# Hyena filter spectra: the even/odd sums on TensorE, one store per side, and the second layer's modulations emitted between the gate blocks

## The chip, the cores and the metric

One core of a Trainium2 chip. The metric is the device time of one execution in microseconds; before, the median of three runs is 1911.43 us (1908.09 to 1912.96). Beside it stands one profiled execution, whose trace all rows below come from.

## The reference

A two-layer diffusion trunk over 1024 latent tokens and 256 context tokens of width 1024. Layer 0 mixes neighbourhood attention and a bidirectional gated DeltaNet behind one input projection. Layer 1 is an order-2 Hyena layer: two long convolutions whose filters come from a small network. Only a part of it is touched here:

```python
def hyena_filters(length, w1, b1, f1, w2, b2, f2, w3):
    ...
    hid = jnp.sin(f2 * (hid @ w2 + b2))
    h = (hid @ w3).astype(jnp.float32).reshape(length, HY_ORDER, HY_DIRS, HY_W)
    ...
    h = h * jnp.exp(-t * decay)[:, None, None, :]
    return h * lax.rsqrt(jnp.sum(h * h, axis=0, keepdims=True) + EPS)

def long_conv(u, h_fwd, h_bwd, skip):
    ...
    hf = jnp.fft.rfft(h_fwd, n=n, axis=0)
    hb = jnp.fft.rfft(h_bwd, n=n, axis=0)
```

Each layer also has a modulation, `m = silu(cvec) @ mod_w + mod_b`, split into shift, scale and gate, and layer 0 a gate path, `silu(px[..., OFF_Z:])`.

## The kernel before, in words

The program is recorded through a scheduling layer that orders each engine's instructions itself, by priority and by its own estimate of when operands are ready; every engine then executes its row in that order. The work of the change lies in `start` (from L317), the first fifth of the program.

**Filter blocks.** For each of 8 channel blocks cb and 2 orders o, so 16 blocks, `filter_pair` (L1259) makes the filters `fh` from the hidden layer by TensorE, multiplies them by the decay on VectorE and normalises them. `filter_block` (L1299) forms the sum and the difference of the forward and the backward filter, folds them into even and odd parts with VectorE and GpSimd, and transposes them with TensorE into `fx` (`xT` in the code). `filter_spectrum` (L1323) is a discrete Fourier transform by matrix products, for a cosine side (0) and a sine side (1). Per side a product `e[:, 0]` of the even samples and a product `e[:, 1]` of the odd ones go into one PSUM bank, and four smaller products into a second bank `r`. ScalarE copies `e[:, 0]` to SBUF (L1340), VectorE makes its sum and its difference with `e[:, 1]` (L1341, L1342), then adds and subtracts the first two parts of `r` (L1343, L1344); ScalarE copies the rest (L1345, L1349). Both sides of a block lie in one SBUF tile `G`, of which there is one; two stores (L1350, L1351) take it to `g_d`, where the second layer reads it much later. The spectra's banks come from pool psf, of three.

**Fill.** With the lowest priority, so that it fills gaps, `start` also records the last four blocks of layer 0's modulation (em), eight gate blocks z0 to z7 (`zblock`, L475) and the twelve blocks of layer 1's modulation, om0 to om11 (`mod_block`, L200). A z block loads 512 KB of weights, ScalarE makes a high part and a negated copy of them, a DMA of GpSimd's queue adds the weights onto the negated copy to give the low part (`load_split` with add, L145), 24 products follow, and ScalarE (L486) and VectorE (L487) empty the bank. A modulation block loads two tiles of 512 KB, makes 8 narrow products, has ScalarE copy the result (L213), and then either transposes it (om0 to om7) or makes one more product (om_g, L224), to which VectorE adds a bias row that SP has just loaded (L226, L227) before a store (L228). All fill shares one PSUM bank (pool psz) and the weight places wraw, whi and wlo, two of each.

**What follows.** `layer0_in` for the second half of the tokens (transposes `xtp1`, VectorE's `xmod`), then `project` (L408): `gates` (L564) makes products `ab` with the small weights `wab`, which are loaded through the same places, and `dn_front` makes the DeltaNet projections `dn` (weights `wdn`).

Of the kernel before, what the change touches and what calls it, by code (L numbers as in the profile page):

```python
# [10 lines left out]
F32 = mybir.dt.float32  # L11
# [3 lines left out]
AF = mybir.ActivationFunctionType  # L15
ALU = mybir.AluOpType
# [4 lines left out]
P = 128  # L21
# [26 lines left out]
Z_EARLY = range(8)  # L48
# [13 lines left out]
class Kernel:  # L62
# [44 lines left out]
    def mm3(self, ps, ws, xs, start, stop):  # L107
        nc = self.nc
        (wh, wl), (xh, xl) = ws, xs
        nc.tensor.matmul(ps, wh, xh, start=start, stop=False)  # L110
        nc.tensor.matmul(ps, wh, xl, start=False, stop=False)  # L111
        nc.tensor.matmul(ps, wl, xh, start=False, stop=stop)  # L112
# [204 lines left out]
    def start(self, st, sh, h):  # L317

        nc, ap = self.nc, self.ap
        psp = self.pool(st, "fpsg", bufs=2, space=bass.MemoryType.PSUM)  # L320
        pst = self.pool(st, "fpst", bufs=2, space=bass.MemoryType.PSUM)
        psf = self.pool(st, "fpsf", bufs=3, space=bass.MemoryType.PSUM)
        self.psg = self.pool(st, "psz", bufs=1, space=bass.MemoryType.PSUM)
        mp = self.pool(st, "mp")
        fc = self.pool(st, "fc")
        self.mod_setup(mp)
        fw = self.pool(st, "fw", bufs=2)
        self.wraw = self.pool(sh, "wraw", bufs=2, side="right")
        self.wsp = self.pool(sh, "wsp", bufs=2, side="right")
        self.ev = self.pool(sh, "ev", bufs=3, side="right")  # L330
        self.hpool(sh, h, 0, 512)
        self.hpool(sh, h, 2, LC)
        self.pending = [None, None]
        with ExitStack() as s1:
            fa = self.fa = self.pool(s1, "fa", side="right")
            hid = [fa.tile([P, L], F32R, name="fhh"), fa.tile([FFN, L], F32R, name="fhl")]
            self.ffn(mp, fw, psp, *hid)
            for j in range(8):
                if j == CONST_AT:
                    w3 = [self.load_w3(0)]  # L340
                    fil = hid, *self.filter_setup(fc)
                self.mod_block(mp, "em", j, self.cols0, None, pst)
            xs = self.load_x(0)
            for cb in range(KT):
                if cb == X_AT:
                    self.layer0_in(xs, psf, h[0], 0, "f")
                    with self.tc.high_priority(offset=-LOW):
                        for j in range(8, 12):
                            self.mod_block(mp, "em", j, None, self.gate_d[0:1, :])
                        for zb in Z_EARLY:  # L350
                            self.zblock(h, zb, (0,), add=True)
                        for j in range(12):
                            self.mod_block(mp, "om", j, self.cols1, self.gate_d[1:2, :])
                if cb == X2_AT:
                    self.layer0_in(self.load_x(2), psf, h[2], 2, "f")
                if cb == X1_AT:
                    xs = self.load_x(1)
                self.filter_pair(cb, w3.pop(0), fil, pst, psp, psf, fw)
                if cb + 1 < KT:
                    w3.append(self.load_w3(cb + 1))  # L360
            self.flush(0)
        self.hpool(sh, h, 1, 512)
        self.layer0_in(xs, pst, h[1], 1)
        self.flush(1)
# [877 lines left out]
    def filter_setup(self, fc):  # L1242

        nc, ap = self.nc, self.ap
        trow = self.fa.tile([P, L], F32, name="trow")
        nc.sync.dma_start(trow, ap["trow"])
        ndel = fc.tile([P, KT], F32, name="ndel")
        nc.sync.dma_start(ndel, ap["ndelta"])
        skip = fc.tile([P, 2, KT], F32, name="skip")
        nc.sync.dma_start(skip, ap["skip"])  # L1250
        mats = self.load_dft(fc, ("a0", "a1", "b0", "b1", "co", "so", "cc", "ss0", "ccn"))
        return trow, ndel, skip, mats

    def load_w3(self, cb):
# [68 lines left out]
    def filter_spectrum(self, cb, o, xTs, mats, psf, fw):  # L1323
        nc = self.nc
        nm = f"{cb}_{o}"
        G = fw.tile([P, 2, 10, P], F32, name="G" + nm, tag="G", bufs=1)
        v = nc.vector
        for side in (1, 0):
            xT = xTs[side]
            e = psf.tile([P, 2, 2, P], F32, name=f"fb0{nm}_{side}", tag="f")  # L1330
            r = psf.tile([P, 4, P], F32, name=f"fb1{nm}_{side}", tag="f")
            m0, m1, mo, mc = ("a0", "a1", "co", "cc") if side == 0 else ("b0", "b1", "so", "ss0")
            self.dft([e[:, 0]], mats[m0], [xT[:, 0:2, :]])
            self.dft([e[:, 1]], mats[m1], [xT[:, 2:4, :]])
# [7 lines left out]
            v.tensor_tensor(Gs[:, 5::4, :], t, e[:, 1], ALU.subtract)  # L1342
            v.tensor_tensor(Gs[:, 0:2, :], Gs[:, 8:10, :], r[:, 0:2], ALU.add)  # L1343
            v.tensor_tensor(Gs[:, 2:4, :], Gs[:, 8:10, :], r[:, 0:2], ALU.subtract)  # L1344
            nc.scalar.copy(Gs[:, 6:8, :], r[:, 2:4])  # L1345
            if side == 0:
                b2 = psf.tile([P, P], F32, name=f"fb2{nm}", tag="f")
                self.dft([b2], mats["ccn"], [xT[:, 6, :], xT[:, 8, :]])
                nc.scalar.copy(G[:, 0, 8, :], b2)  # L1349
        nc.sync.dma_start(self.g_d[o, cb][:, 0:16, :].rearrange("p (a b) c -> p a b c", a=2), G[:, :, 0:8, :])  # L1350
# [312 lines left out]
class Conv:  # L1663
# [284 lines left out]
```

## Time and profile before

| | us |
|---|---|
| median of the timed runs | 1911.43 |
| the profiled execution | 1918.28 |
| span of its trace, first to last instruction | 1916.5 |
| mean granted TensorE clock | 0.955 of full |
| first and last instruction on a spectrum's bank | 85.0 and 383.9 |
| z products, first z block to last modulation product | 111.4 to 349.1 |
| first product with wab, first DeltaNet product | 384.0, 394.9 |

PE is TensorE's products, PEld its weight loads, DVE VectorE, ACT ScalarE, POOL GpSimd, SP the engine whose queue issues most DMAs. Busy time of PE includes products that ran at a lower granted clock and so took longer. A product of fp32 operands is two instructions in the trace. In a row of waits, the left side waited for the right; in a row of the timeline the square brackets say how long the engine had been idle and what ended it. A helper records many operations at one line (L116 for products, L105 and L102 for splits), so groups are told apart by their tiles.

### The profile page before, as it was taken

The page shows a single profiled execution, that of the slowest core. Times are in us where ns is not written, and L with a number is a line of the kernel's source. Part 1 is how long each engine was busy: PE and PEld are TensorE (multiplying, and loading weights), DVE is VectorE, ACT ScalarE, POOL GpSimd, SP SyncE. Part 2 cuts the span into 40 slices and gives each one's busy share as a digit, 9 for nine tenths or more (in the row PEclk, how much of TensorE's full clock was granted, in tenths as well). Part 3 has the DMA queues.
Part 4 walks back from the last instruction along what each step waited for, and adds up shares of the span by engine and source line. Part 5 has one row for each costly group of instructions (what it writes and reads, how often), then busy time and mean ns, then how long its engine had stood idle before and what let it go on. Part 6 is the DMA issues. An engine that isn't in the chain of part 4 may idle for free.

```text
span 1916.5 us, 30316 instructions
## 1 busy us (share of the span) xinstructions
PE 1744.8 (91%) x11124; PEld 1417.4 (74%) x11124; DVE 1405.9 (73%) x2818; ACT 836.7 (44%) x1817; POOL 627.8 (33%) x878
## 2 busy tenths in 40 slices
PE   6798988799989897999987999989999999999898
PEld 2466755678877686888876787778888778888686
DVE  5899988746658554655565765659899989999876
ACT  4557574445535342333344544544334434434321
POOL 0665445422295768721035400330000000000410
PEclk9889988999999998999998999999999999999999
DMA  8535545213424366434489872643343442443343
GB/s 288 173 110 152 158 162 177 98 62 102 158 73 138 122 209 229 150 122 160 150 228 207 228 204 85 185 116 90 105 111 85 106 111 68 111 128 110 106 132 136
DMA packets 131934, 270.50 MB, mean 141 GB/s; under 512 B 43929, under 2 KB 65961, under 8 KB 129738
## 3 DMA queue, kind: packets, MB, share of 16 engines
q1 hardware_dynamic: 122330, 233.45, 37.6%
q0 software_dynamic: 9456, 35.13, 9.6%
q8 instruction: 87, 1.43, 0.3%
q14 instruction: 61, 0.50, 0.1%
HBM read 192.50 MB, written 76.03 MB: 140 GB/s over the span
## 4 chain that ended last, share of the span: by engine, by line
PE 58%; DVE 21%; DMA 8%; POOL 4%; ACT 3%; issue 3%; SPq 1%; DVEq 0%; ACTq 0%; POOLq 0%
PE hx L116 6%; PE fo L116 4%; PE hg L116 3%; PE pa L116 3%; PE hu L116 3%; PE nv L116 2%; DVE ff L1160 2%; PE nq L116 2%; PE z L116 2%; PE pv L116 2%; PE pq L116 2%; PE nk L116 2%; PE do L116 2%; POOL sub L755 2%; POOL Xb L757 2%
## 5 line engine op out<-in xcount | busy, mean ns | idle before, releaser
L112 PE MATMUL dn<-hh,wdn_lo 128*128 128x512 f32 (+1 forms) x256 | 96.0, 376 | 5.9 <-POOL wdn_lo L105 5.9
L652 DVE SCALAR_TENSOR_TENSOR dacc<-dpad,convw,dacc 128x1024 f32<-128x1024 f32 (+1 forms) x80 | 83.7, 1078 | 23.8 <-ACT dacc L650 19.0
L116 PE MATMUL hx<-h1l,w1x_hi 128*128 128x512 f32 x256 | 101.1, 395 | 0.0
L116 PE MATMUL hx<-h1h,w1x_hi 128*128 128x512 f32 x256 | 101.0, 395 | 0.0
L116 PE MATMUL hx<-h1h,w1x_lo 128*128 128x512 f32 x256 | 100.9, 394 | 0.0
L111 PE MATMUL dn<-hl,wdn_hi 128*128 128x512 f32 (+1 forms) x256 | 95.7, 374 | 0.0
L110 PE MATMUL dn<-hh,wdn_hi 128*128 128x512 f32 (+1 forms) x256 | 95.6, 374 | 0.0
L755 POOL TENSOR_TENSOR sub<-Lb,Xb 80x31 f32<-80x31 f32 (+15 forms) x124 | 80.2, 647 | 34.9 <-DMA Lb<-lsc_d 21.2
L757 POOL TENSOR_TENSOR Xb<-Xb,sub 80x31 f32<-80x31 f32 (+15 forms) x124 | 82.3, 664 | 8.4
L1051 ACT ACTIVATE pr<-pr,st 128x640 f32<-128x640 f32 (+1 forms) x64 | 51.4, 803 | 64.9 <-DVE st L1050 64.3
L112 PEld LDWEIGHTS dn<-hh,wdn_lo 128*128 128x128 f32 x256 | 49.4, 193 | 14.9 <-POOL wdn_lo L105 6.1
L1171 ACT COPY fx<-fx_ps 128x512 f32<-128x512 f32 (+1 forms) x96 | 43.5, 483 | 30.9 <-PE fx_ps L121 27.6
L121 PE MATMUL fx_ps<-ident,ff 128*128 128x128 f32 x288 | 51.2, 305 | 5.8 <-ACT fx L1171 3.6
L1280 PE MATMUL fh<-fhh,w3s 128*128 128x512 f32 x64 | 38.9, 611 | 18.4 <-DVE fh L1282 18.4
L110 PEld LDWEIGHTS dn<-hh,wdn_hi 128*128 128x128 f32 x256 | 49.5, 193 | 7.9
L111 PEld LDWEIGHTS dn<-hl,wdn_hi 128*128 128x128 f32 x256 | 49.3, 193 | 8.1 <-issue 0.5
L116 PEld LDWEIGHTS hx<-h1h,w1x_hi 128*128 128x128 f32 x256 | 48.1, 188 | 9.0
L116 PEld LDWEIGHTS hx<-h1l,w1x_hi 128*128 128x128 f32 x256 | 48.1, 188 | 8.9
L116 PEld LDWEIGHTS hx<-h1h,w1x_lo 128*128 128x128 f32 x256 | 48.2, 188 | 8.9
L1304 POOL TENSOR_TENSOR fp<-fh,fh 128x1024 f32<-128x1024 f32 x16 | 39.4, 2461 | 41.6 <-ACT fh L1290 25.2
L121 PEld LDWEIGHTS fx_ps<-ident,ff 128*128 128x128 f32 x288 | 37.5, 155 | 19.9 <-ACT fx L1171 6.6
L116 PE MATMUL hu<-h1h,w1u_hi 128*128 128x512 f32 x128 | 51.3, 401 | 0.8 <-ACT hpu L1631 0.8
(570 smaller groups left out, 5952.2 us busy)
## 6 DMA issues: line engine op xcount, KB each, us to landing
hG<-g_d SPq DMA_DIRECT2D x16, 1088.0 KB
g_d<-G SPq DMA_DIRECT2D x16, 1024.0 KB
em_w<-in_em_w SPq DMA_DIRECT2D x24, 512.0 KB
om_w<-in_om_w SPq DMA_DIRECT2D x24, 512.0 KB
wz_raw<-in_w0z SPq DMA_DIRECT2D x16, 512.0 KB
w1x_raw<-in_w SPq DMA_DIRECT2D x16, 512.0 KB
w1x_lo<-in_w POOLq DMA_DIRECT2D x16, 512.0 KB, 7.7
wdn_raw<-in_w0dn SPq DMA_DIRECT2D x12, 512.0 KB
```

Source lines behind the costliest of these rows:

```text
L110: nc.tensor.matmul(ps, wh, xh, start=start, stop=False)
L111: nc.tensor.matmul(ps, wh, xl, start=False, stop=False)
L112: nc.tensor.matmul(ps, wl, xh, start=False, stop=stop)
L116: ins = self.nc.tensor.matmul(*args, **kw)
L121: ins = self.nc.tensor.transpose(out, x, self.ident)
L652: nc.vector.scalar_tensor_tensor(acc[:, t0:t0 + n], pad[:, o + j:o + j + n], cw[:, blk, j:j + 1], acc[:, t0:t0 + n], ALU.mult, ALU.add)
L755: nc.gpsimd.tensor_tensor(tv, Lb[:, j + 1:, j:j + 1].broadcast_to([80, m, c]), Xb[:, j:j + 1, 0:c].broadcast_to([80, m, c]), ALU.mult)
L757: nc.gpsimd.tensor_tensor(Xb[:, j + 1:, 0:c], Xb[:, j + 1:, 0:c], tv, ALU.subtract)
L1051: nc.scalar.activation(pr[:, :n], pr[:, :n], AF.Exp, bias=st[:, 0:1], scale=-1.0, accum_out=st[:, 1:2])
L1171: nc.scalar.copy(out[:, j0:j0 + m, :].rearrange("p a b -> p (a b)"), ps[:, :m * P])
L1280: nc.tensor.matmul(ps, ws[:, od, :], hh[:, sl], start=True, stop=False)
L1304: nc.gpsimd.tensor_tensor(pp[:, :L], hf[:, :L], hb[:, :L], ALU.add)
```

## The change

Three edits. In `filter_spectrum` the sum and the difference of the even and the odd product are formed in PSUM: `e[:, i]` accumulates the even product and then the odd one with the matrix `a1` (or `b1`) for i = 0, and with its negative for i = 1. Two negated matrices are made once. ScalarE copies one part of both results straight to G and the other to `t`, and VectorE keeps the two operations with `r`. G is a tile per side, each stored on its own. In `start`, two modulation blocks of layer 1 are recorded ahead of each of the first six gate blocks, not all twelve behind the eighth.

```diff
-                        for zb in Z_EARLY:
+                        for i, zb in enumerate(Z_EARLY):
+                            for j in range(2 * i, min(2 * i + 2, 12)):
+                                self.mod_block(mp, "om", j, self.cols1, self.gate_d[1:2, :])
                             self.zblock(h, zb, (0,), add=True)
-                        for j in range(12):
-                            self.mod_block(mp, "om", j, self.cols1, self.gate_d[1:2, :])
...
+        for name in ("a1", "b1"):
+            mats[name + "n"] = fc.tile([P, 1, P], F32, name=f"dft_{name}n")
+            nc.scalar.activation(mats[name + "n"], mats[name], AF.Copy, scale=-1.0)
...
-        G = fw.tile([P, 2, 10, P], F32, name="G" + nm, tag="G", bufs=1)
...
-            self.dft([e[:, 0]], mats[m0], [xT[:, 0:2, :]])
-            self.dft([e[:, 1]], mats[m1], [xT[:, 2:4, :]])
+            for i, m in enumerate((m1, m1 + "n")):
+                self.mm(e[:, i], mats[m0][:, 0, :], xT[:, 0:2, :], start=True, stop=False)
+                self.mm(e[:, i], mats[m][:, 0, :], xT[:, 2:4, :], start=False, stop=True)
...
+            Gs = fw.tile([P, 9 - side, P], F32, name=f"G{nm}_{side}", tag=f"G{side}", bufs=1)
             t = fw.tile([P, 2, P], F32, name=f"fo{nm}_{side}", tag="fo", bufs=1)
-            Gs = G[:, side]
-            nc.scalar.copy(t, e[:, 0])
-            v.tensor_tensor(Gs[:, 4::4, :], t, e[:, 1], ALU.add)
-            v.tensor_tensor(Gs[:, 5::4, :], t, e[:, 1], ALU.subtract)
-            v.tensor_tensor(Gs[:, 0:2, :], Gs[:, 8:10, :], r[:, 0:2], ALU.add)
-            v.tensor_tensor(Gs[:, 2:4, :], Gs[:, 8:10, :], r[:, 0:2], ALU.subtract)
+            nc.scalar.copy(t, e[:, :, 1])
+            nc.scalar.copy(Gs[:, 4:6, :], e[:, :, 0])
+            v.tensor_tensor(Gs[:, 0:2, :], t, r[:, 0:2], ALU.add)
+            v.tensor_tensor(Gs[:, 2:4, :], t, r[:, 0:2], ALU.subtract)
             nc.scalar.copy(Gs[:, 6:8, :], r[:, 2:4])
...
-        nc.sync.dma_start(self.g_d[o, cb][:, 0:16, :].rearrange("p (a b) c -> p a b c", a=2), G[:, :, 0:8, :])
-        nc.sync.dma_start(self.g_d[o, cb][:, 16, :], G[:, 0, 8, :])
+            nc.sync.dma_start(self.g_d[o, cb][:, 8 * side:8 * side + 8, :], Gs[:, 0:8, :])
+            if side == 0:
+                nc.sync.dma_start(self.g_d[o, cb][:, 16, :], Gs[:, 8, :])
```

The scheduler then orders every engine's row anew. Line numbers after the change are one to four higher. On PE, one side of a spectrum before (channel block 2, order 0, sine side; `fb0` is the bank e, `fb1` the bank r, `fx` the transposed folds):

```order
L116 MATMUL fb02_0_1_2084<-fx2_0_1_1803,dft_b0_275 128x256
L116 MATMUL fb02_0_1_2084<-fx2_0_1_1803,dft_b1_277 128x256
L116 MATMUL fb12_0_1_2085<-fx2_0_1_1803,dft_so_281 128x128 x4
L116 MATMUL fb12_0_1_2085<-fx2_0_1_1803,dft_b1_277 128x128
L116 MATMUL fb12_0_1_2085<-fx2_0_1_1803,dft_ss0_285 128x128 x2
```

and after (channel block 3, where the rows also stand together):

```order
L116 MATMUL fb03_0_1_2409<-fx3_0_1_2208,dft_b0_275 128x256
L116 MATMUL fb03_0_1_2409<-fx3_0_1_2208,dft_b1_277 128x256
L116 MATMUL fb03_0_1_2409<-fx3_0_1_2208,dft_b0_275 128x256
L116 MATMUL fb03_0_1_2409<-fx3_0_1_2208,dft_b1n_291 128x256
L116 MATMUL fb13_0_1_2410<-fx3_0_1_2208,dft_so_281 128x128 x4
L116 MATMUL fb13_0_1_2410<-fx3_0_1_2208,dft_b1_277 128x128
L116 MATMUL fb13_0_1_2410<-fx3_0_1_2208,dft_ss0_285 128x128 x2
```

Two products became four into the same bank; the bank r is as it was.

Further down PE's row, at the end of the filter stage before, the last transposes `xtp1_7`, the last spectrum and the first products with `wab` (`ab0`):

```order
L401 MATMUL xtp1_7_3673<-ident_63,x0_6_2879 128x128
L401 MATMUL xtp1_7_3673<-ident_63,x0_7_2883 128x128
L116 MATMUL fb17_1_0_3702<-fx7_1_0_3545,dft_co_279 128x128 x4
L116 MATMUL fb17_1_0_3702<-fx7_1_0_3545,dft_a0_271 128x128
L116 MATMUL fb17_1_0_3702<-fx7_1_0_3545,dft_cc_283 128x128 x2
L116 MATMUL fb27_1_3719<-fx7_1_0_3545,dft_ccn_287 128x128 x2
L574 MATMUL ab0_3768<-hh0_189,wab_3734 32x512
L574 MATMUL ab0_3768<-hl0_190,wab_3734 32x512
```

The same place after the change, behind the last spectrum and om11's two products (`om_ps11` above, `om_g11` here):

```order
L402 MATMUL xtp1_7_3737<-ident_63,x0_4_2915 128x128
L402 MATMUL xtp1_7_3737<-ident_63,x0_5_2919 128x128
L402 MATMUL xtp1_7_3737<-ident_63,x0_6_2923 128x128
L402 MATMUL xtp1_7_3737<-ident_63,x0_7_2927 128x128
L224 MATMUL om_g11_1035<-om_p11_1033,sel_164 1x256
L110 MATMUL z5_0_1048<-hh0_189,wz5_0_hi_1043 128x512
L111 MATMUL z5_0_1048<-hl0_190,wz5_0_hi_1043 128x512
L112 MATMUL z5_0_1048<-hh0_189,wz5_0_lo_1044 128x512
```

The gate block z5 stands where `ab0` stood; z6 follows z5's 24 products at once, then the 48 products `ab`, then z7, then the first `dn`.

ScalarE's row at the same place before, from the last filter copies to the first evacuations of `ab` (`abT`) and the second DeltaNet weights:

```order
L1345 COPY G7_1_3682<-fb17_1_1_3684 128x256
L102 CAST hh1_3608<-xmod1_7_3678 128x512
L1345 COPY G7_1_3682<-fb17_1_0_3702 128x256
L1349 COPY G7_1_3682<-fb27_1_3719 128x128
L577 COPY abT0_3785<-ab0_3768 32x512
L577 COPY abT512_3808<-ab512_3791 32x512
L587 ACTIVATE alog_3837<-alog_3837 128x8
L577 COPY abT1024_3831<-ab1024_3814 32x256
L102 CAST wdn8_hi_4028<-wdn8_raw_4026 128x1024
```

and after (`zt5` empties z5's bank, `wz7_0_hi` and `wz7_0_lo` prepare z7's weights, `hh1` is the high part of the projections' input):

```order
L102 CAST hh1_3672<-xmod1_6_3733 128x512
L102 CAST hh1_3672<-xmod1_7_3742 128x512
L155 CAST wz7_0_hi_1115<-wz7_0_raw_1113 128x1024
L487 ACTIVATE zt5_0_1073<-z5_0_1048 128x512
L154 ACTIVATE wz7_0_lo_1116<-wz7_0_raw_1113 128x1024
L102 CAST wab_3802<-wab_raw_3800 128x8x16
L487 ACTIVATE zt6_0_1109<-z6_0_1084 128x512
L102 CAST wdn4_hi_3966<-wdn4_raw_3964 128x1024
L487 ACTIVATE zt7_0_1145<-z7_0_1120 128x512
L578 COPY abT0_3853<-ab0_3836 32x512
L578 COPY abT512_3876<-ab512_3859 32x512
L102 CAST wdn8_hi_4096<-wdn8_raw_4094 128x1024
```

Between the last copy for the input and the first `abT` stand now the weights of z7, three evacuations of gate blocks, `wab` and the first DeltaNet weights.

More of the change, by code (lines that the diff above doesn't have):

```diff
@@ L1348, in filter_spectrum @@
                 self.dft([b2], mats["ccn"], [xT[:, 6, :], xT[:, 8, :]])
-                nc.scalar.copy(G[:, 0, 8, :], b2)
-        nc.sync.dma_start(self.g_d[o, cb][:, 0:16, :].rearrange("p (a b) c -> p a b c", a=2), G[:, :, 0:8, :])
-        nc.sync.dma_start(self.g_d[o, cb][:, 16, :], G[:, 0, 8, :])
+                nc.scalar.copy(Gs[:, 8, :], b2)
+            nc.sync.dma_start(self.g_d[o, cb][:, 8 * side:8 * side + 8, :], Gs[:, 0:8, :])
+            if side == 0:
+                nc.sync.dma_start(self.g_d[o, cb][:, 16, :], Gs[:, 8, :])
     def load_wout(self, w, pool, ap, name, gate, order, lo_eng=(None,), ahead=0):
```

## The prediction

> **What bounds the kernel now.** I read the totals first, then the busy time by stretch, since the change touches only the first fifth of the program, the stage that makes the filter spectra.
>
> ```profile
> PE 1744.8 (91%) x11124; PEld 1417.4 (74%) x11124; DVE 1405.9 (73%) x2818; ACT 836.7 (44%) x1817; POOL 627.8 (33%) x878
> ```
>
> Over the whole program TensorE is the bound. The stretches say what the average hides. Columns: the stretch, its length, then busy time and instructions of PE, PEld, DVE, ACT, POOL, the granted clock, the DMA share and GB/s. 60 us is where the first spectra's folds begin, 164.8 the store of the fourth of 16 filter blocks, 384.3 the last filter matmul; at 394.9 the first DeltaNet projection starts.
>
> ```profile
> 60.00:164.80 104.80, 86.60 (x440) 60.18 (x441) 100.47 (x208) 65.35 (x118) 67.96 (x75) 0.85 0.46 133
> 164.80:384.30 219.50, 190.11 (x1129) 141.24 (x1128) 186.19 (x418) 119.18 (x241) 107.77 (x129) 0.89 0.45 149
> 384.30:394.90 10.60, 10.60 (x57) 6.09 (x56) 0.92 (x3) 1.81 (x5) 1.17 (x8) 0.96 0.37 127
> 394.90:420.00 25.10, 25.10 (x136) 21.01 (x135) 11.67 (x21) 11.31 (x20) 5.45 (x2) 1.00 0.20 63
> ```
>
> In the first stretch (call it A) VectorE is the bound: 100.5 of 104.8 us, 96%. In the second (B) neither is full: PE 190.1 of 219.5 us (87%) at a clock of 0.89, DVE 186.2 (85%). From 384.3 on PE never rests. So what the stage saves counts only if it lets 394.9, the start of that full stretch, come earlier. I therefore date two points: F, the end of the last filter matmul (384.3 now), and S, the start of the projections (394.9, so F + 10.6 now).
>
> What PE waited for in B (time, times, longest):
>
> ```profile
> PE fb L116 <- DVE G L1342: 9.6, 5, 2.9
> PE fh L1280 <- DVE fh L1282: 7.1, 3, 3.1
> PE fb L116 <- ACT G L1345: 4.3, 2, 3.9
> ```
>
> 13.9 of its 29.4 idle us (219.5 - 190.1) are waits for a spectrum's PSUM bank to be emptied.
>
> **The butterflies.** Each side of a block loses two VectorE operations of four and gains two accumulated products on TensorE.
>
> ```profile
> 60.00:164.80 104.80, 24.63 (x160) 21.01 (x160) 11.98 (x32) 6.32 (x20) 0.85 0.46 133
> 164.80:384.30 219.50, 79.42 (x480) 67.24 (x480) 35.36 (x96) 19.17 (x58) 0.89 0.45 149
> ```
>
> These are the instructions on the spectra's PSUM tiles alone (PE, PEld, DVE, ACT). DVE's 128 are the four per side; half of them is 11.98/2 = 6.0 us in A and 35.36/2 = 17.7 us in B. The price on PE:
>
> ```profile
> 185.94 1.13 PE L116 MATMUL fb<-fx,dft_b 128*128 128x256 f32 x4
> 186.91 1.05 PE L116 MATMUL fb<-fx,dft_so 128*128 128x128 f32 x8
> ...
> 358.13 1.22 PE L116 MATMUL fb<-fx,dft_ccn 128*128 128x128 f32 x4 [3.94 <-ACT G L1345]
> 359.80 2.08 PE L116 MATMUL fb<-fx,dft_b 128*128 128x256 f32 x4 [0.44 <-DVE G L1342]
> 361.66 1.91 PE L121 MATMUL fx_ps<-ident,ff 128*128 128x128 f32 x8
> ```
>
> Two 256-column products are four instructions: 186.91 - 185.94 = 0.97 us start to start, or 361.66 - 359.80 = 1.86 us right after PE had waited 3.94. One such pair is added per side, two per block: 1.94 us a block, 3.7 at the slow pace. For the 12 blocks of B that is 23.3 us, for the 4 of A 7.8. In A it falls into PE's 18 idle us.
>
> The slow pace is the clock. The Trainium skill, "TensorE: Matmul & The Clock Gate", Part 1, says that the clock has two states, full and half, and drops to half after about 3.4 us without work; the rows above agree (1.86 against 0.97 behind a 3.94 us wait). By that rule a denser PE in B gets its clock back, which I take up as the first rival; the sum here goes by rows: PE's 0.89 in B may stay or rise to 1.
>
> ScalarE gets one more copy per side:
>
> ```profile
> L1345 ACT COPY G<-fb 128x256 f32<-128x256 f32 x32 | 12.0, 374 | 19.0 <-DVE G L1344 16.2 <-issue 2.5 <-PE fb L116 0.3
> ```
>
> 32 x 0.374 = 12 us on an engine that is busy 119 of 219.5 us in B: hidden by its idle time, and if it were not, at most 12. It also empties the first bank by two copies (0.75 us) instead of a copy and two VectorE operations, so the 13.9 us of waits for banks should mostly go. The two negated matrices are two copies of 128x128 (0.27 us each by the nearest row), in a gap of 2.46 us where ScalarE waits for VectorE:
>
> ```profile
> L1349 ACT COPY G<-fb x16: 243/272/295, 98.6 to 384.6; 128x128 f32<-128x128 f32 x16
> 21.12 0.63 ACT L1239 ACTIVATE hid<-hid 128x512 f32<-128x512 f32 x1 [2.46 <-DVE hid L1238]
> ```
>
> **A store per side.** 16 more issues on SP at 0.38 us each, 6 us over 324 on a queue that mostly waits. The chain of waits shows what the single G buffer costs:
>
> ```profile
> L1350 SPq DMA_DIRECT2D g_d<-G x16: 371/377/461, 98.8 to 384.8; - x16
> ...
> 345.89 3.27 DMA g_d<-G
> 374.44 5.53 DMA g_d<-G
> ```
>
> The last two are 8.8 us near the end of B; with a buffer per side, stored while the other side is still being made, both should go. They are idle PE time, so they are inside the 29.4, not on top of it.
>
> **The reordering.** By the order of PE, before had all eight gate blocks z0 to z7 and the twelve modulations om0 to om11 done inside the filter stage. After, z0 to z4 and om0 to om9 are; om10, om11, six of the eight transposes xtp1 and z5, z6, z7 stand behind the last filter matmuls. In A three z blocks leave (z0 to z2), whose evacuations cost DVE 0.68 us each; B loses three z and gets three (five before, five after), and gives up four om blocks, 4 x (1.35 + 0.5), and six xtp groups, 6 x 0.45.
>
> ```profile
> 60.00:384.30 324.30, 16.17 (x192) 5.72 (x192) 4.51 (x12) 0.87 0.45 143
> 343.76 0.59 PE L224 MATMUL om_g<-om_p,sel 128*1 128x256 f32 x2
> 371.75 0.60 PE L401 MATMUL xtp<-ident,x 128*128 128x128 f32 x4
> L487 DVE SCALAR_TENSOR_TENSOR zt<-zt,z x16: 666/683/689, 128.8 to 988.9; 128x512 f32<-128x512 f32 x16
> ```
>
> (First row: the modulations' products alone, 16.17 us for 12.)
>
> *Stretch A*: DVE 100.5 - 6.0 - 3 x 0.68 = 92.4 us; at the same 96% that is 96.4 us, 8.4 less. *Stretch B*: PE 190.1 + 23.3 - 7.4 - 2.7 = 203.3 us at the old clock, 203.3 x 0.89 = 181 at full clock; DVE 186.2 - 17.7 = 168.5 or a little less. PE is now the longer, whatever the clock. I take half the clock back, 192 us. Of the 29.4 idle us the 13.9 for the banks go, and I let 5 of the 7.1 for fh go, since VectorE has less to do; 10.5 stay. B is then 202.5 us, 17 less. Bounds: 181 + 5 = 186 (33 less) and 203.3 + 29.4 = 233 (13 more). So F moves by -8.4 - 17 = **-25 us**, to 359.
>
> *The tail*, from F to S, was 10.6 us and now holds work with little to overlap. The fill shares one PSUM bank (pool psz), so each piece waits for the last to be emptied.
>
> ```profile
> 330.65 0.24 SPq L228 DMA_DIRECT2D gate_d<-om_gr  x1
> ...
> 357.05 0.23 SPq L228 DMA_DIRECT2D gate_d<-om_gr  x1
> DVE om_gr L227 <- DMA om_gr<-in_om_brow: 3.3, 1, 3.3
> 191.15 0.50 PE L110 MATMUL z<-hh,wz_hi 128*128 128x512 f32 x1 [1.65 <-DVE zt L487]
> 196.73 0.83 PE L116 MATMUL fb<-fx,dft_co 128*128 128x128 f32 x6
> L155 ACT CAST wz_hi<-wz_raw x8: 1030/1047/1092, 83.4 to 197.0; 128x1024 fp32r<-128x1024 f32 x8
> L486 ACT ACTIVATE zt<-z x16: 578/596/617, 126.4 to 988.3; 128x512 f32<-128x512 f32 x16
> L102 ACT CAST wab<-wab_raw x1: 312/312/312, 334.3 to 334.3; 128x128 fp32r<-128x128 f32 x1
> L105 DVE TENSOR_TENSOR wab<-wab_raw,wab x1: 278/278/278, 336.0 to 336.0; 128x128 fp32r<-128x128 f32 x1
> 388.49 0.58 ACT L577 COPY abT<-ab 32x512 f32<-32x512 f32 x1 [3.57 <-PE ab L574]
> 384.35 8.49 PE ab L574 x38
> 392.84 0.99 PE ab_tp L580 x8
> 393.83 1.27 PE ab L574 x10
> ```
>
> The four gate rows of om8 to om11 left 26.4/3 = 8.8 us apart, with filter work in between as cover: each needs a product, a copy, a second product, a small load (3.3 us) and an add before the bank is free. In the changed program om11's bias row has the same SBUF place as its own partial sum, so that load starts only after its second product. I put om10's add at F + 5.5 (1 us of product, a 3.3 us load behind z6's weights on SP, the add) and om11's 8.8 later: z5 starts at F + 14. A z block takes 196.73 - 191.15 = 5.6 us. Between z5 and z6: ScalarE first makes wz7_hi (it stands ahead of zt5 in its row and needs z5's weights done), 1.05, then zt5 0.6, VectorE 0.68, hand-overs 0.5: 2.8. Then z6 5.6; wab, whose place z6's weights hold, 0.31 + 0.28 and 0.4 of hand-overs, 1.0; ab 9.8 (8.49 + 1.27); z7 5.6; the abT copy behind zt7 0.6 + 0.58 + 0.4, 1.6; the first ab_tp 0.5. Sum 14 + 5.6 + 2.8 + 5.6 + 1.0 + 9.8 + 5.6 + 2.1 = 46.5: **+35.9 us** against 10.6. Bounds: the work alone, 5.7 + 16.8 + 9.8 + 0.5 = 32.8 (+22), and 50 (+39).
>
> **Sum**: -8.4 - 17 + 35.9 = +10.5 us, on a profiled run of 1918.3 us (span 1916.5), 0.4% above the median of the three timed runs, 1911.4. Behind S the order of PE is the same and PE is full, so the shift passes on. On the median: 1911.4 + 10.5 = **1922**. About 0.3%, 6 us, is what a measurement of this kernel tells from no change.
>
> **The rivals.** *PE packs tightly*: in B the clock comes back whole and waits vanish. Stretch B at 186 us, tail at 41: -8.4 - 33 + 30 = -11, about **1900**. For it: PE is at 100% from 394.9 on, where its order was planned just as densely, and by the skill's rule the clock recovers whole. Against it: in B the other engines keep it waiting now, and in the tail there are new waits. It decides where F falls below about 349, which needs PE busy for 94% of B at full clock (181/193). *The two halves cancel*: B at 192 to 203 with a tail of 41 gives -8.4 - 27.5 + 30.4 = -5.5 to -8.4 - 16.5 + 30.4 = +5.5, **1906 to 1917**. *PE keeps its idle time*: it executes in the planned order, and each misjudged piece holds the queue; B stays near 228 us (192 + 29.4 + some clock): -8.4 + 8 + 36 = +36, **1947**. For it: that B idles now with both engines under 88%. *VectorE was never the bound, so nothing is gained*: A at 96% speaks against it.
>
> **How the numbers follow.** My forecast, a loss of 6 to 25 us with F between 349 and 374, gets 0.43; the larger loss 0.17; cancelling 0.21; tight packing 0.19. Slower by over 0.3%: 0.60, the same 0.21, faster 0.19. The range leaves out the lower half of the fast rival and the end of the largest loss: 1903 to 1944.
>
> **What would show it.** Right: half as many VectorE operations on G; PE fuller than 92% in B and its clock above 0.93; no g_d wait on the chain; F near 359; then some 46 us to the first projection, with z6's wait on zt5 and the wait for om11's row in it. Wrong: z5 following F at once, S ahead of 389, or B still idle by 25 us.

## The result and the profile after

The changed kernel takes 1938.36 us (median of 4 executions, 1932.36 to 1943.27) against 1912.19 us: ratio 1.0138, 95% interval 1.0114 to 1.0162. A second measurement gave 1942.31 against 1910.77, ratio 1.0174 (1.0150 to 1.0199). So it is slower by 26 to 32 us, where 10.5 was forecast; 1938 lies inside the range of 1903 to 1944.

The stretches of the changed kernel, in the columns of the prediction: 150.2 is where the store of the fourth block's second side begins, 366.3 is F, 413.7 is S.

```profile
60.00:150.20 90.20, 76.45 (x421) 52.52 (x420) 81.58 (x168) 51.45 (x106) 54.94 (x63) 0.84 0.42 136
150.20:366.30 216.10, 197.16 (x1146) 150.29 (x1145) 182.10 (x374) 129.12 (x265) 104.32 (x128) 0.92 0.43 136
366.30:413.70 47.40, 38.96 (x188) 25.71 (x180) 11.48 (x21) 14.19 (x25) 13.68 (x20) 0.86 0.45 111
413.70:440.00 26.30, 26.30 (x141) 22.29 (x141) 12.34 (x22) 11.60 (x21) 5.42 (x2) 1.00 0.24 71
```

Stretch A ends 14.6 us earlier than before (150.2 against 164.8), B is 3.4 us shorter (216.1 against 219.5), the tail is 47.4 us against 10.6, and behind S TensorE is full again. VectorE's busy time from 60 us to F fell from 286.7 to 263.7 us, as the removed operations say. In B TensorE is busy for 197.2 us, 91%, at 0.92.

The spectra's PSUM tiles alone, in A and B (PE, PEld, DVE, ACT):

```profile
60.00:150.20 90.20, 34.74 (x192) 29.90 (x192) 6.02 (x16) 8.65 (x28) 0.84 0.42 136
150.20:366.30 216.10, 100.38 (x576) 85.12 (x576) 17.19 (x46) 26.93 (x84) 0.92 0.43 136
```

TensorE spends 135.1 us on them, 31.1 more than the 104.0 of before; VectorE half as much.

What TensorE waited for in B (time, times, longest):

```profile
PE fh L1284 <- DVE fh L1286: 11.3, 4, 3.6
PE fx_ps L121 <- ACT fx L1172: 3.7, 4, 1.2
PE fb L116 <- ACT G L1354: 2.2, 1, 2.2
```

The waits for a spectrum's bank are down from 13.9 to 2.2 us. The waits for the filters' own bank `fh`, of which 5 of 7.1 us were to go, have grown to 11.3 (4.3 in a second trace of before); from 60 us to F they are 15.6 us, against 18.4 and 14.5.

TensorE's timeline in the tail, the rows that begin with a wait:

```profile
372.96 1.94 PE L210 MATMUL om_ps<-om_w,cT 128*32 128x256 f32 x16 [2.62 <-DVE om_gr L227]
379.75 0.80 PE L110 MATMUL z<-hh,wz_hi 128*128 128x512 f32 x1 [2.02 <-DVE om_gr L227]
390.46 0.50 PE L110 MATMUL z<-hh,wz_hi 128*128 128x512 f32 x1 [2.13 <-DVE zt L488]
396.73 0.42 PE L575 MATMUL ab<-hh,wab 128*32 128x512 f32 x1 [0.53 <-DVE wab L105]
412.73 1.06 PE L581 MATMUL ab_tp<-selab,abT 32*128 32x16 f32 x8 [1.14 <-ACT abT L578]
```

The waits that the prediction named are there. z5 starts 13.4 us after F (14 foretold) and z6 10.7 us later (8.4 foretold: z5's first half ran at the slow pace).

### The profile page after: what moved, and what is told of

It reads as the page before. It is cut to its first block, busy times and chain, and to the rows that moved or that the text cites. A ratio compares the mean times of both kernels' runs of the same rounds, so it can differ in the third digit from the quotient of the medians.

```text
span 1930.5 us, 30574 instructions
## 1 busy us (share of the span) xinstructions
PE 1764.4 (91%) x11252; PEld 1437.7 (74%) x11252; DVE 1394.1 (72%) x2754; ACT 846.0 (44%) x1851; POOL 627.2 (32%) x878
## 4 chain that ended last, share of the span: by engine, by line
PE 53%; DVE 12%; DMA 5%; POOL 5%; issue 3%; ACT 2%; SPq 0%; DVEq 0%; ACTq 0%; POOLq 0%
PE hx L116 6%; PE fo L116 4%; PE hg L116 3%; PE pa L116 3%; PE hu L116 2%; PE nv L116 2%; PE pv L116 2%; PE nq L116 2%; PE do L116 2%; PE z L116 2%; POOL Xb L758 2%; PE pq L116 2%; PE nk L116 2%; PE s L116 2%; PE dn L110 2%
## 5 line engine op out<-in xcount | busy, mean ns | idle before, releaser
L758 POOL TENSOR_TENSOR Xb<-Xb,sub 80x31 f32<-80x31 f32 (+15 forms) x124 | 86.5, 697 | 8.4
L112 PEld LDWEIGHTS dn<-hh,wdn_lo 128*128 128x128 f32 x256 | 48.8, 191 | 14.6 <-POOL wdn_lo L105 6.1
L121 PE MATMUL pt<-ident,pr 128*128 128x128 f32 x304 | 46.8, 282 | 11.2 <-ACT pts L1065 6.9
L1172 ACT COPY fx<-fx_ps 128x512 f32<-128x512 f32 (+1 forms) x96 | 45.1, 486 | 21.4 <-PE fx_ps L121 21.0
L121 PEld LDWEIGHTS pt<-ident,pr 128*128 128x128 f32 x304 | 37.5, 145 | 22.0 <-ACT pts L1065 9.0
```

Of the source, the lines that this page charges most:

```text
L121: ins = self.nc.tensor.transpose(out, x, self.ident)
L758: nc.gpsimd.tensor_tensor(Xb[:, j + 1:, 0:c], Xb[:, j + 1:, 0:c], tv, ALU.subtract)
L1172: nc.scalar.copy(out[:, j0:j0 + m, :].rearrange("p a b -> p (a b)"), ps[:, :m * P])
```

## The experiments

Sixteen runs followed, four of them (e0_again, b_same, a3, a4) of an unchanged kernel. F, S and the span are of each one's trace; the median and the ratio to the kernel before are of its timed runs. B is for the butterflies on TensorE, S for the store per side, E for the new emission order; "early" is how many gate blocks the fill holds.

| kernel | edits, early | F | S | span | median | ratio (95%) |
|---|---|---|---|---|---|---|
| before, first trace | -, 8 | 384.3 | 394.9 | 1916.5 | | |
| b_same | -, 8 | 378.4 | 388.7 | 1903.3 | 1909.0 | 1.0001 (0.9987 to 1.0016) |
| after, first trace | BSE, 8 | 366.3 | 413.7 | 1930.5 | 1938.4 | 1.0138 |
| e0_again | BSE, 8 | 360.7 | 408.4 | 1932.2 | 1942.3 | 1.0174 |
| a3 | BSE, 8 | 364.3 | 411.8 | 1932.3 | one run, 1934.1 | |
| a4 | BSE, 8 | 368.5 | 416.2 | 1943.9 | one run, 1945.7 | |
| e1_bfly | BS, 8 | 355.7 | 397.7 | 1916.6 | 1923.8 | 1.0067 (1.0043 to 1.0091) |
| e8_bonly | B, 8 | 358.0 | 395.8 | 1923.8 | 1921.2 | 1.0060 (1.0044 to 1.0076) |
| e2_emit | E, 8 | 390.1 | 401.4 | 1916.5 | 1919.0 | 1.0051 (1.0030 to 1.0072) |
| e3_store | S, 8 | 374.6 | 392.3 | 1910.4 | 1916.3 | 1.0037 (1.0023 to 1.0051) |
| e7_se | SE, 8 | 378.4 | 397.3 | 1918.5 | 1920.3 | 1.0049 (1.0033 to 1.0065) |
| e4_z5 | BSE, 5 | 360.8 | 386.4 | 1917.2 | 1914.5 | 1.0026 (1.0011 to 1.0042) |
| z3 | BSE, 3 | 364.2 | 382.7 | 1925.5 | 1929.2 | 1.0094 (1.0076 to 1.0113) |
| z3v | SE, 3 | 366.4 | 384.7 | 1927.9 | 1931.1 | 1.0115 (1.0087 to 1.0144) |
| f_omfirst | BS, om first, 8 | 366.7 | 418.7 | 1943.5 | 1947.8 | 1.0185 (1.0154 to 1.0216) |
| norow | BSE, 8, no rows | 363.4 | 409.6 | 1944.9 | 1938.0 | 1.0143 (1.0119 to 1.0167) |
| y5 | BS, 5 | 346.6 | 379.5 | 1909.1 | 1921.5 | 1.0056 (1.0025 to 1.0087) |
| h_z5 | -, 5 | 378.2 | 388.4 | 1916.5 | 1916.7 | 1.0022 (1.0003 to 1.0042) |

**The two kernels again.** No edit.

> The changed kernel once more, unchanged, for a second trace and a narrower ratio. Its first trace had the last filter matmul (F) at 366.3 us and the first DeltaNet projection (S) at 413.7, so S came 18.8 us later than the 394.9 of the kernel before, while the timed medians differ by 26. Theory 'the loss is made ahead of S': this trace again has F between 364 and 369 and S between 411 and 417, and the timed difference settles near 19 to 24 us. Rival 'part of the loss arises behind S': S as before, but a timed difference of 26 or more and markers behind S that lie further apart than 19 us.

> The kernel before once more, unchanged, for a second trace of it. Its first trace was of an execution of 1918 us, 7 us above its timed median, with S at 394.9. The single edits measured so far all lie further from before by the timed medians than by S: changed kernel S +13 to +19 but 27 to 31 us, butterflies with stores S +2.8 but 13 us, new order alone S +6.5 but 8, store alone S -2.6 but 5.5. Theory 'the first trace of before was a late one, and S was taken too late by it': this trace has S between 385 and 391 and a span of 1906 to 1912. Rival 'S is right and the other kernels lose behind S': S at 393 to 397 again, and the stretch from S to the end at least 5 us shorter than theirs.

> The changed kernel, unchanged, for a third trace. Theory 'the rest of the timed loss arises in the stretch from the first do to the first hx, whose transfers keep TensorE waiting for a bank more often than before': if the execution takes 1938 us or more, that stretch takes 244 to 250 us and S lies at 408 to 414. Rival 'S itself is later in the slower executions': S at 417 or more, the stretch near 236.

> The changed kernel, unchanged, for a fourth trace; the same two theories as for the third: in an execution of 1938 us or more, either the stretch from do to hx takes 244 to 250 us with S at 408 to 414, or S lies at 417 or later.

The stretches of the kernel before in its second trace, up to the fourth block's store, F and S:

```profile
60.00:162.60 102.60, 86.23 (x433) 59.92 (x433) 97.14 (x205) 63.76 (x116) 65.16 (x74) 0.83 0.45 128
162.60:378.40 215.80, 188.38 (x1129) 140.73 (x1128) 186.59 (x418) 119.35 (x241) 109.49 (x129) 0.89 0.46 151
378.40:388.70 10.30, 10.30 (x57) 5.99 (x56) 0.85 (x3) 1.80 (x5) 1.06 (x8) 0.99 0.38 131
```

The first trace of before was a late one, by 6 us at S and 13 at the end, as b_same's theory had it, though its span is shorter than was expected. e0_again has F and S earlier than either theory said and a timed difference of 32 us, so part of the loss lies behind S. In the mean of two traces of before and four of after, the fourth block's store comes 13.2 us earlier, B is 3.2 shorter, the tail 37.1 longer, S 20.7 later (391.8 to 412.5), and the span grows by 24.8 us, 1909.9 to 1934.7. The last 4 us arise behind S, in the stretch from the first product `do` to the first `hx`: 236.1 and 239.7 us before; 235.0, 246.3, 245.5 and 246.1 after. What TensorE waits for there in the fourth trace of after:

```profile
PE do L116 <- DVE dx L1120: 9.4, 1, 9.4
```

and in its first trace:

```profile
PE do L116 <- DVE dx L1120: 2.9, 2, 2.0
```

One wait of 8.4 to 9.4 us for the bank of `do` is there in three traces of four. What brings it was not tried. A late start alone does not: e8_bonly, with S at 395.8, waits 8.4 us there, norow 7.0, while f_omfirst has the latest S of all and takes 239.1 us for the stretch. The expectations set S against this stretch: in the slowest of the four (a4), both are late, and a3 was faster than the 1938 us from which its theories spoke.

**One edit at a time.** e1_bfly is the changed kernel with the old order, e2_emit and e3_store the kernel before with one edit, e7_se with both of these, e8_bonly with the butterflies alone.

```diff
# e1_bfly, e8_bonly (against after); the reverse is e2_emit, e7_se (against before, e3_store)
-                        for i, zb in enumerate(Z_EARLY):
-                            for j in range(2 * i, min(2 * i + 2, 12)):
-                                self.mod_block(mp, "om", j, self.cols1, self.gate_d[1:2, :])
+                        for zb in Z_EARLY:
                             self.zblock(h, zb, (0,), add=True)
+                        for j in range(12):
+                            self.mod_block(mp, "om", j, self.cols1, self.gate_d[1:2, :])
# e8_bonly too
+        G = fw.tile([P, 2, 9, P], F32, name="G" + nm, tag="G", bufs=1)
...
+            Gs = G[:, side]
...
+        nc.sync.dma_start(self.g_d[o, cb][:, 0:16, :].rearrange("p (a b) c -> p a b c", a=2), G[:, :, 0:8, :])
# e3_store, against before
-            Gs = G[:, side]
+            Gs = fw.tile([P, 10, P], F32, name=f"G{nm}_{side}", tag=f"G{side}", bufs=1)
...
+            nc.sync.dma_start(self.g_d[o, cb][:, 8 * side:8 * side + 8, :], Gs[:, 0:8, :])
```

> The TensorE butterflies and the store per side, with the old emission order (all gate blocks z0 to z7, then om0 to om11). In PE's row all z and om0 to om4 then stand inside the filter stage, and om5 to om10 behind it, each a narrow product, a copy, a second product, a 3.3 us row load and an add through one PSUM bank. Theory 'fill left behind F is what costs': F lies later than in the changed kernel (374 to 380, since more fill stands ahead of it), the tail is 32 to 45 us (six gate rows at some 5 to 7 us), S 408 to 420, so 13 to 25 us slower than before. Rival 'the price is that of TensorE's products, whatever the order': the same time as the changed kernel within 0.3%, with F later than 384. Rival 'the emission order is to blame': no slower than before by over 5 us, S at 395 to 400.

> The new emission order alone, with VectorE's butterflies and the single store of before. In PE's row all the fill then stands ahead of the last filter matmul, as in the kernel before. Theory 'fill left behind F is what costs': no cost here, F at 380 to 388, tail 10 to 12 us, time within 6 us of before. Rival 'the emission order is to blame': at least 15 us slower than before, with z5 to z7 or om10 and om11 waiting on each other inside the stage.

> The store per side alone, with VectorE's butterflies and the old order. In PE's row only om11 then stands just behind the last filter matmul. Theory of the prediction: the two waits for stores at the end of the stage (3.3 and 5.5 us) go, they lie inside PE's idle time, F comes 3 to 9 us earlier, om11 adds 5 to 8 us to the tail: -4 to +6 us net. Rival 'the waits for the single buffer held the whole stage': F 10 us or more earlier and the time at least 6 us shorter than before.

> The store per side and the new emission order together, with VectorE's butterflies. In PE's row all fill then stands ahead of the last filter matmul. Theory 'fill left behind F is what costs': none is left here, so F at 378 to 386, tail 10 to 12, and the time within 6 us of before. Rival 'the edits cost what they cost singly': 8 + 5.5 us, 11 to 16 us slower than before.

> The TensorE butterflies alone, with one tile G and its two stores, and the old emission order. In PE's row om5 to om10 stand behind the last filter matmul, as with the store per side. Theory 'the loss is made by what the butterflies push behind F, and the store per side is a gain inside the stage': waits for stores come back, F 3 to 9 us later than the 355.7 with the store per side, 16 to 24 us slower than before. Rival 'the store per side costs 5 us by itself': 5 to 10 us slower than before, faster than with the store per side.

Up to the fourth block's store, to F and to S in e1_bfly:

```profile
60.00:154.20 94.20, 81.31 (x435) 58.02 (x435) 88.66 (x178) 60.35 (x116) 62.01 (x70) 0.90 0.41 126
154.20:355.70 201.50, 186.68 (x1103) 149.17 (x1102) 169.40 (x358) 123.03 (x258) 97.88 (x123) 0.96 0.46 144
355.70:397.70 42.00, 30.24 (x211) 15.97 (x209) 12.07 (x30) 11.86 (x26) 6.31 (x13) 0.81 0.44 149
```

Its waits for `fh` in the second of these stretches:

```profile
PE fh L1284 <- DVE fh L1286: 2.8, 2, 2.2
```

Up to F, and from F to S, in e7_se:

```profile
60.00:378.40 318.40, 268.11 (x1531) 197.04 (x1532) 277.93 (x610) 178.26 (x347) 165.37 (x193) 0.87 0.45 143
378.40:397.30 18.90, 16.16 (x86) 10.20 (x85) 10.47 (x15) 7.20 (x14) 12.25 (x17) 0.91 0.27 85
```

and the wait that grew most in e2_emit, from 60 us to F:

```profile
PE fh L1280 <- DVE fh L1282: 22.6, 7, 8.4
```

No edit gains, and none costs much: 8 us (E), 5.5 (S), 12 (B), 13 for B and S, 11 for S and E. All three cost 26 to 32, more than the 13 of B and S and the 8 of E. Theory "fill behind F is what costs" is only half the matter. e2_emit has none there, e7_se only the last products of a gate block and three groups of transposes (a tail of 18.9 us, not 10 to 12), and they are still 8 and 11 us slower, beyond the 6 allowed; in e7_se the rival, that the single costs add up, is right. About half of what TensorE's idle time up to F grew by in e2_emit are waits for `fh`: 18.4 and 14.5 us in the two traces of before, 22.6 here. e1_bfly loses the 13 us that the theory gave, but otherwise than it said: the tail of 42.0 us is as foretold, and F comes at least 18 us earlier, S 10. By its trace S is only 5.9 us later than the mean of before and the span 6.7 longer, so half of the timed 13 us is not seen there. e3_store does what the prediction made of it: the waits for stores go, F comes earlier, om11 slides behind F and S stays within the spread of before, at the upper end of the expected -4 to +6. For e8_bonly neither theory's time holds (12 us slower, between the 10 of the one and the 16 of the other); the store per side changes nothing that can be told apart, 1921.2 without it and 1923.8 with it.

What the butterflies cost hangs on the order: about 1940 - 1920 = 20 us over e7_se in the new one, 1923.8 - 1916.3 = 7.5 over e3_store in the old one. Against e1_bfly the new order costs 14.8 us at S in the mean of the four traces, 9.3 of them ahead of F (365.0 against 355.7) and the rest in the tail.

**Emptying the tail.** In e4_z5 five gate blocks are early with three modulations ahead of each, in z3 three with four; z3v is z3 with VectorE's butterflies; f_omfirst records all twelve modulations ahead of the eight gate blocks; norow leaves out two bias rows.

```diff
# e4_z5 (z3: range(3) and 4 * i; z3v: the same on e7_se)
-Z_EARLY = range(8)
+Z_EARLY = range(5)
...
-                            for j in range(2 * i, min(2 * i + 2, 12)):
+                            for j in range(3 * i, min(3 * i + 3, 12)):
# f_omfirst
+                        for j in range(12):
+                            self.mod_block(mp, "om", j, self.cols1, self.gate_d[1:2, :])
+                        for zb in Z_EARLY:
+                            self.zblock(h, zb, (0,), add=True)
# norow
+            if name == "om" and j >= 10:
+                nc.vector.tensor_copy(g, ps[0:1, 0:256])
+            else:
                 nc.sync.dma_start(g, ap[name + "_brow"][0:1, (j - 8) * 256:(j - 7) * 256])
                 nc.vector.tensor_tensor(g, g, ps[0:1, 0:256], ALU.add)
```

> The changed kernel with five early gate blocks in place of eight and three modulations ahead of each: the three halves z5 to z7 go to the projections' stage, 3 x 5.6 = 16.8 us of products. In PE's row z3 and z4 stand behind the last filter matmul, and no modulation but om11's second product. Theory 'the loss is the serial tail': F 358 to 366, tail 25 to 32, S 386 to 395, and of the 18 to 22 us won at S the 16.8 come back in a stage where PE never rests: 0 to 8 us faster than the changed kernel, still 18 to 30 slower than before. Rival 'the loss is the wait for om11's row and the half clock behind it': at least 12 us faster than the changed kernel. Rival 'the projections have room for the three halves': 15 us faster or more, level with before or better.

> The changed kernel with three early gate blocks in place of eight and four modulations ahead of each: in PE's row nothing of the fill stands behind the last filter matmul, and five halves, z3 to z7, go to later stages. Theory 'fill that is left behind F costs its whole serial time, and finds room later': F 352 to 362, tail 10 to 12, S 363 to 374, 20 us earlier than with five early blocks, of which at most the two halves (11 us) come back: 1903 to 1912 us, level with before or up to 6 us faster. Rival 'every half costs its 5.6 us wherever it stands': within 4 us of the kernel with five early blocks (1914.5 us).

> The same with VectorE's butterflies: store per side, new emission, three early gate blocks; PE's row has no fill behind F either. It prices the butterflies alone. Theory 'VectorE bounds the filter stage and TensorE's products help there': F 362 to 375, 8 to 15 us later than with TensorE's butterflies, and the whole 6 to 15 us slower than that kernel. Rival 'the 31 us of added products cost more than VectorE's 24': at least 5 us faster than that kernel.

> The changed kernel with the same work and another emission order: all twelve modulations first, then z0 to z7. In PE's row z3 (half of it) to z7 stand behind the last filter matmul and no modulation. Theory 'the loss is the serial tail of any fill': F 350 to 358, tail 48 to 55 us (five gate blocks of 5.6 with a hand-over of 2 to 3 between them, ab 9.8, abT 2), S 402 to 409: 0 to 10 us faster than the changed kernel. Rival 'the gate rows' loads make the loss': 12 us faster or more.

> The changed kernel without the bias rows of om10 and om11 (left out: the loads and the addition of half of the second layer's gate bias; VectorE copies in place of adding). PE's row is as in the changed kernel but for om11 and the last transposes, which stand a little closer. Theory of the prediction, that each of the two rows holds the one bank of the fill for its 3.3 us load: z5 starts 6 to 8 us after F and not 13.5, the half clock behind it goes (some 3 us), S 7 to 10 us earlier relative to F, and the whole 6 to 10 us faster than the changed kernel. Rival 'the rows are not on the path': within 3 us of it.

Up to F and from F to S in e4_z5:

```profile
60.00:360.80 300.80, 264.94 (x1548) 193.10 (x1548) 259.11 (x545) 180.02 (x370) 167.00 (x191) 0.91 0.41 137
360.80:386.40 25.60, 25.06 (x133) 17.74 (x132) 11.80 (x19) 8.26 (x16) 11.98 (x17) 1.00 0.40 115
```

Two gate blocks stand in this tail, interleaved with `xtp`, and TensorE idles for 0.5 us of it at full clock; in the changed kernel's tail it idles 8.4 us at 0.86. S comes 26.1 us earlier than the mean of after, and behind S, where z5 to z7 now are, the trace takes 8.6 us more (1530.8 against 1522.2). The three halves are 16.8 us of work; between S and the first product `s` TensorE idles 31.7 us against 38 to 41 in after, so part of them fills gaps. Timed, the kernel is 24 to 28 us faster than the changed one. So most of the loss goes, with all three edits in place, once three gate blocks are out of the stage and two of them, with no modulation, stand behind F in place of three and two modulations. The first theory's F, tail and S are all right, but the halves come back at half of what it charged, and the time is that of the third theory. It would fit the second too, which f_omfirst and norow test.

z3 shows where the room ends. Its S is only 3.7 us earlier than e4_z5's, its stretch behind S 12 us longer, and in the stretch from 990 to 1035 us TensorE waits for operands that come from DRAM:

```profile
PE s L116 <- DMA nkh<-nk_d: 12.8, 2, 7.1
PE s L116 <- DMA nkl<-nk_d: 3.3, 2, 2.2
```

In e4_z5 neither of these waits is there. So both its theories fall: two more halves cost 13 us timed (18.5 above before, against 5.5), more than their 11.2 of work, and 8.3 us by the two traces. z3v against z3, up to F, z3v:

```profile
60.00:366.40 306.40, 243.46 (x1424) 174.68 (x1425) 275.63 (x611) 168.38 (x336) 164.44 (x190) 0.86 0.40 133
```

z3:

```profile
60.00:364.20 304.20, 264.88 (x1552) 193.47 (x1553) 258.98 (x547) 178.06 (x368) 164.83 (x190) 0.90 0.40 133
```

16.7 us less of VectorE, 21.4 more of TensorE, and the stretch is 2.2 us shorter; timed the two differ by 1.8 us, and their intervals overlap. Both theories fall: with nothing left behind F, the trade of VectorE's operations against TensorE's products is worth next to nothing. TensorE's idle time up to F fell by 23.6 us, from 62.9 to 39.3, and the added products took 21.4 of it. What TensorE waits for most, from 60 us to F, in z3:

```profile
PE fh L1284 <- DVE fh L1286: 21.5, 10, 4.8
```

and in z3v:

```profile
PE fh L1280 <- DVE fh L1282: 21.7, 7, 7.9
```

The largest wait of the stage is for VectorE's work on the next filters, and in this order lightening VectorE by 6% did not touch it; the waits that went are others, above all one of 12.2 us for the transposed folds `fx` in z3v. In the old order the same trade did: from 60 us to F the waits for `fh` are 21.4 us in e3_store and 11.2 in e1_bfly.

f_omfirst has no modulation in its tail and five gate blocks, and its tail is 52 us as foretold:

```profile
366.70:418.70 52.00, 45.03 (x202) 32.99 (x200) 14.82 (x20) 15.89 (x26) 15.21 (x21) 0.93 0.52 123
```

F did not come earlier (350 to 358 foretold), so it is no faster than the changed kernel. The rows' loads are not needed for the loss. norow says the same from the other side. Three of the rows with a wait in its tail:

```profile
372.02 0.50 PE L110 MATMUL z<-hh,wz_hi 128*128 128x512 f32 x1 [0.50 <-DVE om_gr L227]
375.64 0.69 PE L112 MATMUL z<-hh,wz_lo 128*128 128x512 f32 x1 [2.89 <-DMA wz_lo<-in_w0z]
384.68 0.50 PE L110 MATMUL z<-hh,wz_hi 128*128 128x512 f32 x1 [2.13 <-DVE zt L491]
```

z5 starts 8.6 us after F, 4.8 earlier than in the changed kernel, and then waits 2.89 us for its weights, at half pace after it. The tail is 46.2 us against 47.4, the time the same. The rows were on the path, and the weights stood right behind them: removing the one wait uncovers the other, so the 6 to 10 us of its theory did not come.

**Five early blocks without the new order.** y5 is e1_bfly, h_z5 the kernel before, with `Z_EARLY = range(5)`.

> TensorE's butterflies and the store per side, the old emission order, five early gate blocks (z0 to z4, then om0 to om11); om8 to om10 stand behind the last filter matmul. By the traces so far TensorE's work at full clock is some 29 us more with the TensorE butterflies (1690 against 1661), and the time depends on how much of it idle time and clock take back. Theory 'the new emission order costs some 15 us under the TensorE butterflies, as it did with eight early blocks': 5 to 15 us faster than the kernel with five early blocks and the new order (1914.5), so 1900 to 1910, level with before or better. Rival 'with five early blocks little fill is left, so the order no longer matters': 1911 to 1918.

> The kernel before with five early gate blocks in place of eight: VectorE's butterflies, old order, no fill behind the last filter matmul. Theory 'VectorE bounds the stage, so taking fill from TensorE there gains little and the three halves cost later': F 366 to 378, S 377 to 389, and behind S 13 us more, so within 8 us of before on either side. Rival 'the three halves are free later': 10 us faster than before or more.

The two stretches of y5:

```profile
60.00:346.60 286.60, 260.02 (x1517) 194.96 (x1518) 253.91 (x534) 177.27 (x366) 155.90 (x190) 0.94 0.44 139
346.60:379.50 32.90, 25.98 (x155) 13.92 (x154) 11.76 (x27) 10.96 (x23) 6.22 (x13) 0.82 0.30 98
```

It has the earliest F and S of all, but its nine runs spread from 1904 to 1932 us and its median is no better than e4_z5's, so the theory of a gain of 5 to 15 us falls and the rival is nearer, though 3.5 us too fast. h_z5 is 7 us slower than before: the halves aren't free there, as its theory had it. No version here beats the kernel before.

## Why the prediction was right in direction and too small

**Work at full clock.** Busy time of TensorE times the granted clock, summed over seven stretches of each trace, is 1656 to 1676 us in the seven traces with VectorE's butterflies and 1685 to 1698 in the eleven with TensorE's: 27 more in the mean, near the 31.1 of the prediction (23.3 + 7.8). For the change itself, two traces against four, the span is made up so: +27 work, +3 idle time, -5 lost to the clock, together +25. The clock is given to two places, so a single sum is rough: the two traces of before give 1671 and 1656. The prediction had this price right and its cover wrong.

**Stretch A**, -8.4: measured -13.2, by the fourth store. That less work for VectorE shortens it stands: with TensorE's butterflies the fourth store comes 13.3 us earlier in the old order (154.2 in e1_bfly, 167.5 in e3_store) and 12.4 in the new one (150.5 in the mean of after, 162.9 in e7_se).

**Stretch B**, -17: measured -3.2. This is the step that failed: "I take half the clock back, 192 us", and of 29.4 idle us "10.5 stay". In the four traces of after 18.9 or 19.0 us stay, and TensorE is busy for 193.9 to 197.2 us. Its work was right, 197.2 x 0.92 = 181 us at full clock, as foretold; the clock came back to 0.92 to 0.94, which is 2 to 5 us of the miss, and the idle time, which is 8.4. The waits for the spectra's banks went nearly as foretold (13.9 to 2.2); those for `fh`, of which 5 of 7.1 us were to go "since VectorE has less to do", are 11.2 or 11.3 us in all four traces.

In place of this step the runs show that it holds in the old order and fails in the new one. e1_bfly, with the same butterflies and stores, has a stretch B of 201.5 us at a clock of 0.96 (186.7 x 0.96 = 179 us of work), with 2.8 us of waits for `fh`, and F at 355.7: close to the 202.5 and the 359 of the forecast. The prediction counted the reordering inside the stage as work that moves in and out, and put the waits of the new order at nothing. Why TensorE finds the bank of `fh` full for longer in that order stays open; other fill stands in the stage, too. A and B together were forecast at -25 and came to -16.4.

**The tail**, +35.9: measured +37.1, the waits where they were put. It was argued that om11's row held z5; the row was on the path, but norow shows that it could be taken away without any gain: a wait for z5's weights, which the forecast did not name, stood behind it.

**Behind S** nothing was to happen; 4 us did, in a stretch in which TensorE already idled for 23 us. The forecast had 10.5; A -4.8, B +13.8, the tail +1.2 and these 4 make it 24.7, and the traces have 24.8. The timed runs lie 1 to 7 us further apart than the traces. Single executions of the same kernel differ by 10 us and more, and the traces of after and e0_again are each of the fastest execution of their measurement; whether that is all of it stays open.

**The baseline.** The profiled execution that the sum was made on was 6 us late at S against the second trace; that shifts no term by more than 4 us (B: 219.5 and 215.8).

**The rivals.** That PE keeps its idle time (1947) came nearest: B was to be 228 us, it was 216, and 18.9 of the 29.4 idle us stayed. Tight packing and cancelling fell with the idle time of B. "VectorE was never the bound" had been put aside by A's 96%. For A that stands; for the whole stage the worth of a lighter VectorE hangs on the order: z3 against z3v shows a gain of 2.2 us at F from 16.7 us less of VectorE, e1_bfly against e3_store one of 18.9 from 21.6 less, though five more modulations stand behind F there.

## What to carry to other kernels

Price moved work on the engine that bounds the whole program, 27 us here, and ask where its idle time is to take it up: a wait counts as cover only if what ends it changes in the order that will run. In one order here the largest wait had the same length with and without the relieved operations, in the other it was half as long. Look in the new order for filler that slides behind the last work it was meant to hide under: there it runs one piece at a time through one bank, and taking three gate blocks out of the stage brought S 26 us earlier, though they cost 9 us later. Edits that cost 5 to 13 us each cost 26 to 32 together, so measure such edits apart and together.

## What the runs showed of the hardware

The clock fell behind waits shorter than I had expected. In the changed kernel's tail a wait of 2.62 us was followed by the 16 narrow products of om11 in 1.94 us; in its third trace the same products took 1.07 us, behind a wait of 2.68. The Trainium skill, "TensorE: Matmul & The Clock Gate", Part 1, states that the clock falls after an idle window of about 3.4 us, and that the window runs freely; no wait in the four tails of the changed kernel reached 3.4 us, the longest was 3.19, so a shorter one was enough here. Which wait does it changes from run to run, as these two show; and behind the 2.13 us ahead of z6 the products start 0.23 us apart in the first trace, and in the third trace 0.43 us from the third product on. So the mean clock of the same tail is 0.86 in three traces and 0.93 in the other, whose row from F to S is

```profile
364.30:411.80 47.50, 37.33 (x190) 25.15 (x189) 11.92 (x21) 14.46 (x25) 14.09 (x20) 0.93 0.45 113
```

and its length is the same within 0.3 us: what the clock gave back, the waits took (10.2 us idle against 8.4).
